# Hybrid GLA/MLA encoder layer: reciprocals by a small transpose, another order of loads and first products, and a root on GpSimd

## The chip, the cores and the metric

The kernel runs on one core of a Trainium2 chip. TensorE (PE) multiplies matrices, with weight loads (PEld) beside it; VectorE (DVE), ScalarE (ACT) and GpSimd (POOL) work on tiles in on-chip memory (SBUF) or in the matrix accumulators (PSUM); SyncE (SP) issues most of the DMA transfers, ACT a few. Each engine works through its own list in order and waits on semaphores. The metric is the time of one execution on the device in microseconds, as the median of several runs.

## The reference

One encoder layer over 2048 tokens of width 1024:

```python
h = x @ w_in
o_a = gla_branch(...)      # chunked gated linear attention, 4 heads, width 512
o_b = mla_branch(...)      # softmax attention on compressed keys and values, 4 heads, width 512
x = layer_norm(alpha * x + concatenate([o_a, o_b]) @ w_out, ln_g, ln_b)
```

In `mla_branch`, each query block takes `p = softmax(s)` over all 2048 keys, multiplies by the values and by `silu(gate)`. Everything is float32. The kernel keeps that precision by splitting each factor into a high part, rounded to TensorE's format, and the rest, and by taking three products (high by high, high by low, low by high) in `mm3`.

## The kernel before

The program has several sweeps over the tokens (input projections, the two scans of linear attention, the projections of the softmax branch), then the softmax attention, then the output projection with the layer norm. Only the last two are touched by the change. Tokens are taken in 16 chunks of 128 (`NCH`), queries in 4 blocks of 512 (`QB`).

**Attention.** There are 16 blocks `i`, one for each head and query block; block 15 is the last, block 14 the last but one. A block has eight steps `j`, each with two key tiles. `scores` fills a PSUM tile of `pS` (two buffers), ACT copies it (`copy`), VectorE keeps the running maximum (`smax`); after step 7, `tmax`, `rmax` and `bmax` turn the maximum into a row by transposes on TensorE with a reduction on VectorE between; `sub` (VectorE), `exp`, `phi` (ACT), `plo` (POOL) make the weights and `pv` multiplies them with the values into the bank `o`. `acc` sums the weights, and `tot` puts the sums into one tile; `tsum` transposes them on TensorE (tile `sx`), and `rcp` (VectorE) makes the reciprocals `rc`, 128 by 4. For block 15, `tot` is a copy out of the bank of the pool `pA`, and `tsum` and `y` borrow the banks `pA` and `pO` (`close`). `oh` and `ol` split `o`, `y` multiplies with the value projection, `yc` copies and stores the result in `ob_s`.

The reciprocals go to DRAM (`r_s`) in one of two ways. `keep` (L1639 to L1641) stores `rc` straight from its 128 by 4 tile, element by element, on ACT's queue. `turn` and `rows` (L1643 to L1654) first transpose it on TensorE into the bank `pA`, have ACT copy the four rows of 128, and store these on SP's queue. Before the change only block 15 takes the second way.

**Output stage.** For each chunk, `load` (L1839) fetches the two mixer outputs, the gate and the reciprocals; `hi` and `lo` (ACT, POOL) split the factors, `gate` (POOL, L1859) multiplies the softmax branch by gate and reciprocals, `load_res` (L1872) fetches the residual input `xr`; `part` and `product` take 48 matrix products of 512 columns; `residual` (VectorE, L1926) adds `alpha * xr` out of the bank, and `finish` (L1929) does the layer norm: mean and variance, `(r - mean) * gain` in two halves, the reciprocal root in `rsqrt` (logarithm and exponential on ACT, L432 and L433, then four one-column steps on VectorE, L438 to L441, which sharpen it), multiply-and-add in two halves (L1941) and two stores on SP's queue. Even chunks from 2 on use the banks `mb` and `x` (rows `pmb` and `px`), odd ones and chunks 0 and 1 use `pS` (rows `po`); so an even chunk can't start before `residual` has emptied the bank of the even chunk before it. The last chunk, 15, is taken in pieces of 512, 256 and 256 columns.

**What sets the order.** Attention and the first chunks are put in order by hand: `put(place, fn, ...)` gives each step a place, in units of a step `j` (`end` is 128, the end of the scores), and all engines follow the sorted list. The products of chunks 0 and 1 for each of the 8 weight tiles stand at `end + out["part"][k]`, `tmax` of block 15 at `end + 0.26`. Behind that list, chunks 4 to 15 run in a loop in which ACT, POOL and SP keep the written order (`fixed`, `LATE_ORDER`), while a planner orders TensorE and VectorE by priority and by when it expects inputs to be ready. In the loop, `split(c + 2)` is `hi`, `lo` and `gate` of a later chunk, `load(c + 4)` its loads, and the remaining steps of blocks 14 and 15 are appended behind chunks 4, 5 and 7.

Of the kernel before, what the change touches and what calls it, by code (L numbers as in the profile page):

```python
# [13 lines left out]
ALU = mybir.AluOpType  # L14
# [8 lines left out]
NCH = S // P  # L23
# [63 lines left out]
    tot=11.2,  # L87
    tsum=12.04,
    rcp=13.55,
    keep=14.21,  # L90
    oh=12.34,
    ol=12.99,
    y=16.55,
    yc=16.9,
# [20 lines left out]
    w_hi=0.74,  # L115
    w_step=6.49,
    w_lo=4.26,
    part=(1.05, 2.03, 5.45, 8.05, 10.24, 17.37, 21.96, 27.24),
    whole=(24.99, 55.73),
    sum=(38.16, 49.19),  # L120
# [234 lines left out]
class K:  # L355
# [77 lines left out]
        nc.scalar.activation(y, l, AF.Exp, scale=-0.5)  # L433
        return u, y, t, w, r

    def rsqrt_b(self, u, y, t, w, r):
        nc = self.nc
        nc.vector.tensor_tensor(t, y, u, ALU.mult)  # L438
        nc.vector.tensor_tensor(w, t, y, ALU.mult)
        nc.vector.tensor_scalar(t, w, -0.5, 1.5, ALU.mult, ALU.add)  # L440
        nc.vector.tensor_tensor(r, t, y, ALU.mult)  # L441
        return r

    def rsqrt(self, pool, u, n, name):
        return self.rsqrt_b(*self.rsqrt_a(pool, u, n, name))


    def load_w(self, pool, stage, src, ncols, tag, k, lo_eng="dve", hi_eng="act", bufs=None):
# [1037 lines left out]
    def attention(self):  # L1486
        tc, nc = self.tc, self.nc
        mm = nc.tensor.matmul
        V, G, Ac = nc.vector, nc.gpsimd, nc.scalar
        NP = NKT // 2  # L1490
        with ExitStack() as ctx:
# [6 lines left out]
            nb = len(blocks)  # L1498
# [140 lines left out]
            def keep(i):  # L1639
                h, b = blocks[i]  # L1640
                Ac.dma_start(self.r_s[b][:, h].rearrange("o (e p) -> p (o e)", p=P), stt[i]["rc"])  # L1641
# [46 lines left out]
            op = OutProj(self, ctx, qp, bp, sp, pS, pM, pX, pO, pA)  # L1688
            first = [dict(c=c) for c in range(4)]
# [4 lines left out]
            def put(place, fn, *a):  # L1694
                todo.append((place, len(todo), fn, a))
# [7 lines left out]
            for i in range(nb):  # L1703
                for j in range(NP):
                    t = NP * i + j
# [11 lines left out]
            out = PLACE_OUT  # L1717
            end = NP * nb
            for k in range(NK):
                if k < PRE_W:  # L1720
                    v = NP * (PRE_BLOCK + k)
                    hi, lo = v + out["pre_hi"], v + out["pre_lo"]
                else:
                    hi = end + out["w_hi"] + (k - PRE_W) * out["w_step"]
                    lo = hi + out["w_lo"]
                if k == 0:
                    put(hi - 6, op.fetch_w, k)
                put(hi, op.split_hi, k)
                put(lo, op.split_lo, k)
                if k + 1 < NK:  # L1730
                    put(lo + 0.01, op.fetch_w, k + 1)
                else:
                    put(max(lo, end + 26) + 0.02, op.load_ln)
                put(end + out["part"][k], lambda k: [op.part(o, k) for o in first[:2]], k)
            for c, o in enumerate(first):
                put(end + (out["lo1"][c - 1] + 0.01 if c else out["hi0"][0] - 6), op.load, o)
                for j in range(2):
# [16 lines left out]
            rest = {c: o for c, o in enumerate(first)}  # L1754

            def load(c):
                if c < NCH:
                    rest[c] = dict(c=c)
                    op.load(rest[c])

            def split(c):
                if c < NCH:
                    op.hi(rest[c], 0)
                    op.lo(rest[c], 0)
                    op.gate(rest[c])
                    op.hi(rest[c], 1)
                    op.lo(rest[c], 1)
# [17 lines left out]
                    op.finish(rest[c])  # L1785
            for c in range(4, NCH):
                with fixed():
                    split(c + 2)
                    load(c + 4)
                    if 4 < c < NCH - 1:  # L1790
                        op.load_res(rest[c + 1])
                    op.product(rest[c])
                    op.finish(rest[c])
                with self.after(*last.values()), fixed():
                    if c == 4:
                        keep(nb - 2)
                    for f in {4: (tot, oh, ol), 5: (tsum, rcp), 7: (turn, y, rows, yc)}.get(c, ()):
                        f(nb - 1)


class OutProj:
# [127 lines left out]
    def finish(self, o):  # L1929
        kern, nc, sm = self.k, self.nc, self.sm  # L1930
        V, Ac = nc.vector, nc.scalar
        c, rr = o["c"], o["rr"]
        mv = sm.tile([P, 2], F32, tag="mv", name=f"mv{c}")
        u = sm.tile([P, 1], F32, tag="u", name=f"u{c}")
        V.bn_aggr(mv, o["bn"])
        V.tensor_scalar(u, mv[:, 1:2], LN_EPS, None, ALU.add)
        for n in range(2):
            V.scalar_tensor_tensor(rr[:, n], rr[:, n], mv[:, 0:1], self.ln[0][:, n], ALU.subtract, ALU.mult)
        rs = kern.rsqrt(sm, u, 1, f"ln{c}")
        for n in range(2):  # L1940
            V.scalar_tensor_tensor(rr[:, n], rr[:, n], rs, self.ln[1][:, n], ALU.mult, ALU.add)  # L1941
            nc.sync.dma_start(kern.out[c * P:(c + 1) * P, n * 512:(n + 1) * 512], rr[:, n])
# [68 lines left out]
```

## Time and profile before

| What | Value |
|---|---|
| Median of 3 runs | 1307.95 us (1307.42 to 1308.66) |
| Profiled execution's own time | 1308.66 us |
| Its span | 1306.3 us |
| TensorE busy | 1280.9 us, 98% |
| VectorE busy | 958.2 us, 73% |
| ScalarE busy | 812.8 us, 62% |
| GpSimd busy | 783.6 us, 60% |

All rows give microseconds from the start of the span. A row of the timeline has start, duration, engine, line and operation, output and inputs, shapes and count, and in square brackets the idle time before it with what ended it; "x4" means that so many alike instructions are merged. In a list of waits, the three numbers are the sum, the count and the longest. A matmul of 512 columns is listed with its full length through the pipeline (0.39 us), while the next one follows in less; start to start is what counts. SPq and ACTq are the queues on which SP and ACT issue transfers: the duration of such a row is that of the issue, not of the transfer.

### The profile page before, as it was taken

What the parts mean: (1) busy time and instruction counts of PE and PEld (TensorE: products, weight loads), DVE (VectorE), ACT (ScalarE), POOL (GpSimd) and SP (SyncE); (2) the same over time, 40 slices, a digit from 0 to 9 for tenths busy, and PEclk for the clock granted to TensorE, in tenths of its full rate; (3) what the DMA queues carried; (4) which work ended last, traced back from release to release, by engine and by line L of the source; (5) the groups of instructions that cost most, each with busy time, mean ns of one, the idle gap of its engine ahead of it and who ended that gap; (6) DMA issues with size and microseconds to landing.
All of it is one profiled execution on the core that took longest, in us unless ns stands there. A gap on an engine that the chain in (4) does not pass through costs nothing.

```text
span 1306.3 us, 19979 instructions
## 1 busy us (share of the span) xinstructions
PE 1280.9 (98%) x7081; PEld 1130.9 (87%) x7081; DVE 958.2 (73%) x1712; ACT 812.8 (62%) x1339; POOL 783.6 (60%) x494
## 2 busy tenths in 40 slices
PE   7999999999999999999999999999999999999997
PEld 7999999999989999999788888888888887887786
DVE  6967774645675455555798888888888888377998
ACT  6764656655575656655688878888888888411110
POOL 0143333242457666672298888889999999934441
PEclk9999999999999999999999999999999999999999
DMA  8131313122475565565501111122123110376563
GB/s 285 61 101 54 94 49 91 55 68 79 132 249 170 193 214 181 178 210 170 145 1 41 41 42 41 41 57 65 58 81 97 41 41 12 119 234 175 195 197 109
DMA packets 107820, 145.81 MB, mean 112 GB/s; under 512 B 17251, under 2 KB 62695, under 8 KB 107721
## 3 DMA queue, kind: packets, MB, share of 16 engines
q1 hardware_dynamic: 99128, 142.41, 35.6%
q0 software_dynamic: 672, 2.10, 0.4%
q8 instruction: 56, 0.92, 0.3%
q10 hardware_dynamic: 7920, 0.03, 0.3%
q14 instruction: 44, 0.35, 0.2%
HBM read 94.14 MB, written 50.36 MB: 111 GB/s over the span
## 4 chain that ended last, share of the span: by engine, by line
PE 83%; DMA 4%; DVE 3%; ACT 2%; POOL 1%; issue 1%; SPq 1%; DVEq 0%; POOLq 0%; ACTq 0%
PE pS L1520 4%; PE o L419 4%; PE o L420 4%; PE o L421 4%; PE pS L1522 4%; PE pS L1523 4%; PE pS L1521 4%; PE pS L1524 4%; PE ipa L419 4%; PE ipa L421 4%; PE ipa L420 4%; PE pz L420 2%; PE pz L419 2%; PE pz L421 2%; PE ipg L419 2%; PE ipg L420 2%
## 5 line engine op out<-in xcount | busy, mean ns | idle before, releaser
L371 POOL TENSOR_TENSOR pl<-s,ph 128x1024 fp32r<-128x1024 f32 x128 | 306.5, 2414 | 58.3 <-ACT ph L365 54.5
L1542 DVE TENSOR_TENSOR rm<-pS,rm 128x512 f32<-128x512 f32 x210 | 144.8, 690 | 36.5 <-ACT s L1529 31.2
L1529 ACT ACTIVATE s<-pS 128x1024 f32<-128x1024 f32 x128 | 131.4, 1027 | 60.6 <-PE pS L1524 51.3
L1566 DVE TENSOR_TENSOR s<-s,mb 128x1024 f32<-128x1024 f32 x128 | 151.2, 1213 | 9.5 <-PE mb L1560 9.3
L1029 POOL TENSOR_TENSOR Us<-Us,cw 128x512 f32<-128x512 f32 x16 | 18.5, 1157 | 227.2 <-DVE Us L1027 175.3
L365 ACT ACTIVATE ph<-s 128x1024 fp32r<-128x1024 f32 x128 | 135.2, 1057 | 17.1 <-PE o L421 16.5
L1570 ACT ACTIVATE s<-s 128x1024 f32<-128x1024 f32 x128 | 131.4, 1050 | 13.7 <-DVE s L1566 13.7
L419 PE MATMUL ipa<-wah,xah 128*128 128x384 f32 (+1 forms) x384 | 131.1, 342 | 6.7 <-ACT wah L365 6.7
L421 PE MATMUL ipa<-wah,xal 128*128 128x384 f32 (+1 forms) x384 | 125.5, 327 | 0.0
L420 PE MATMUL ipa<-wal,xah 128*128 128x384 f32 (+1 forms) x384 | 125.2, 326 | 0.0
L1520 PE MATMUL pS<-qh,ckvT_h 128*128 128x512 f32 x256 | 102.6, 401 | 0.8 <-DVE rm L1542 0.4
L419 PE MATMUL o<-ph,vh 128*128 128x512 f32 x256 | 101.0, 395 | 0.0
L421 PE MATMUL o<-ph,vl 128*128 128x512 f32 x256 | 99.8, 390 | 0.0
L1522 PE MATMUL pS<-qh,ckvT_l 128*128 128x512 f32 x256 | 99.8, 390 | 0.0
L1523 PE MATMUL pS<-rh,krs 128*128 128x512 f32 x256 | 99.8, 390 | 0.0
L1524 PE MATMUL pS<-rl,krs 128*128 128x512 f32 x256 | 99.7, 389 | 0.0
L1521 PE MATMUL pS<-ql,ckvT_h 128*128 128x512 f32 x256 | 99.7, 389 | 0.0
L420 PE MATMUL o<-pl,vh 128*128 128x512 f32 x256 | 99.7, 389 | 0.0
L1593 DVE TENSOR_TENSOR ap<-ap,s 128x512 f32<-128x512 f32 x120 | 83.0, 692 | 2.7 <-ACT s L1570 0.7
L371 POOL TENSOR_TENSOR ol<-of,oh 128x512 fp32r<-128x512 f32 x32 | 42.9, 1343 | 66.9 <-ACT oh L365 66.9
L419 PEld LDWEIGHTS ipa<-wah,xah 128*128 128x128 f32 x384 | 73.7, 192 | 7.9 <-ACT wah L365 7.0
L419 PE MATMUL pz<-xch,wzh 128*128 128x256 f32 x256 | 74.8, 292 | 0.0
(325 smaller groups left out, 3858.0 us busy)
## 6 DMA issues: line engine op xcount, KB each, us to landing
xcf<-xT_dram SPq DMA_DIRECT2D x16, 512.0 KB, 4.9
xr<-x_dram SPq DMA_DIRECT2D x16, 512.0 KB, 6.6
out_dram<-rr SPq DMA_DIRECT2D x32, 256.0 KB, 2.0
xaf<-xT_dram SPq DMA_DIRECT2D x14, 512.0 KB, 4.2
oib<-oi_s SPq DMA_DIRECT2D x16, 256.0 KB, 4.4
qdb<-qd_s SPq DMA_DIRECT2D x16, 256.0 KB, 4.6
SU<-su_s SPq DMA_DIRECT2D x16, 256.0 KB, 4.9
ub<-u_s SPq DMA_DIRECT2D x16, 256.0 KB, 4.7
```

The costliest lines, as they stand in the source:

```text
L365: return nc.scalar.activation(dst, src, AF.Copy).ins
L371: return e.tensor_tensor(dst, src, hi.bitcast(F32), ALU.subtract).ins
L419: mm(out, ah, bh, start=start, stop=False)
L420: mm(out, ah, bl, start=False, stop=False)
L421: mm(out, al, bh, start=False, stop=stop)
L1520: mm(ps[:, e], kh, qh, start=True, stop=False)
L1521: mm(ps[:, e], kh, ql, start=False, stop=False)
L1522: mm(ps[:, e], kl, qh, start=False, stop=False)
L1523: mm(ps[:, e], kr, rh, start=False, stop=False)
L1524: mm(ps[:, e], kr, rl, start=False, stop=True)
L1542: V.tensor_tensor(d["rm"], src[:, e], d["rm"], ALU.max)
L1566: V.tensor_tensor(s, s, d["mb"][:, None, :].to_broadcast([P, 2, QB]), ALU.subtract)
```

## The change

1. The first two groups of products of the output stage, those of chunks 0 and 1 with weight tile 0, get places of their own: chunk 0's at `end + 0.255`, just before `tmax` of block 15 (0.26), chunk 1's stays at `end + 1.05`. Both stood at 1.05.
2. In the loop over chunks, `load_res` of the next chunk stands before `split` and `load` instead of behind them, for chunks 5 to 14. On SP's queue, one transfer passes four.
3. The reciprocals of block 14 no longer take `keep` but `turn` and `rows`, behind chunk 4: a transpose on TensorE into the bank `pA` after `tot` of block 15, a copy of 4 by 128 on ACT after `oh` of block 15, a store on SP's queue. One transfer of ACT's queue is gone.
4. The four one-column root steps of the last chunk run on GpSimd instead of VectorE.

```diff
@@ PLACE_OUT
+    part0=(0.255, 1.05),
     part=(1.05, 2.03, 5.45, 8.05, 10.24, 17.37, 21.96, 27.24),
@@ class K
-    def rsqrt_b(self, u, y, t, w, r):
-        nc = self.nc
-        nc.vector.tensor_tensor(t, y, u, ALU.mult)
-        nc.vector.tensor_tensor(w, t, y, ALU.mult)
-        nc.vector.tensor_scalar(t, w, -0.5, 1.5, ALU.mult, ALU.add)
-        nc.vector.tensor_tensor(r, t, y, ALU.mult)
+    def rsqrt_b(self, u, y, t, w, r, eng=None):
+        e = eng or self.nc.vector
+        e.tensor_tensor(t, y, u, ALU.mult)
+        e.tensor_tensor(w, t, y, ALU.mult)
+        e.tensor_scalar(t, w, -0.5, 1.5, ALU.mult, ALU.add)
+        e.tensor_tensor(r, t, y, ALU.mult)
         return r
-    def rsqrt(self, pool, u, n, name):
-        return self.rsqrt_b(*self.rsqrt_a(pool, u, n, name))
+    def rsqrt(self, pool, u, n, name, eng=None):
+        return self.rsqrt_b(*self.rsqrt_a(pool, u, n, name), eng)
@@ attention: the list by places
-                put(end + out["part"][k], lambda k: [op.part(o, k) for o in first[:2]], k)
+                for o, place in zip(first, out["part0"]):
+                    put(end + (out["part"][k] if k else place), op.part, o, k)
@@ attention: the loop over chunks
             for c in range(4, NCH):
                 with fixed():
+                    if 4 < c < NCH - 1:
+                        op.load_res(rest[c + 1])
                     split(c + 2)
                     load(c + 4)
-                    if 4 < c < NCH - 1:
-                        op.load_res(rest[c + 1])
                     op.product(rest[c])
                     op.finish(rest[c])
                 with self.after(*last.values()), fixed():
-                    if c == 4:
-                        keep(nb - 2)
-                    for f in {4: (tot, oh, ol), 5: (tsum, rcp), 7: (turn, y, rows, yc)}.get(c, ()):
-                        f(nb - 1)
+                    for f, i in {4: ((tot, 1), (turn, 2), (oh, 1), (ol, 1), (rows, 2)), 5: ((tsum, 1), (rcp, 1)),
+                                 7: ((turn, 1), (y, 1), (rows, 1), (yc, 1))}.get(c, ()):
+                        f(nb - i)
@@ OutProj.finish
-        rs = kern.rsqrt(sm, u, 1, f"ln{c}")
+        rs = kern.rsqrt(sm, u, 1, f"ln{c}", nc.gpsimd if c == NCH - 1 else V)
```

## The prediction

> **What bounds the kernel now.** I read the page first, then the waits of TensorE, then the chain of waits and the DMA issues of the stage that the diff touches.
>
> ```profile
> span 1306.3 us, 19979 instructions
> ...
> PE 1280.9 (98%) x7081; PEld 1130.9 (87%) x7081; DVE 958.2 (73%) x1712; ACT 812.8 (62%) x1339; POOL 783.6 (60%) x494
> ```
>
> TensorE is busy for 98% of the span, so only its gaps are to be had. Its list of waits from 1095 us to the end has two lines, one at the change from attention to output stage, one inside the output stage:
>
> ```profile
> PE pmb L419 <- DVE rr L1926: 3.1, 1, 3.1
> PE mx L1548 <- DVE rm L1542: 1.0, 1, 1.0
> ```
>
> The long one, in the chain that ended last (start, duration, what):
>
> ```profile
> 1185.22 14.26 DMA gr<-gm_s
> ...
> 1199.50 0.92 SPq L1853
> ...
> 1200.46 7.79 DMA xr<-x_dram
> ...
> 1208.38 0.70 DVE rr L1926
> ...
> 1209.22 0.47 PE pmb L419
> ```
>
> TensorE waits for VectorE to empty chunk 6's bank, VectorE for the residual input xr of chunk 6, and this stands on SP's queue behind the loads of chunk 9, which crawl. Why they crawl is in the DMA issues of 1180 to 1206 us, and what the gap leaves behind in the table of windows (PE busy, then other engines, then granted clock):
>
> ```profile
> r_s<-rc ACTq DMA_DIRECT2D x1, 2.0 KB, 11.0
> ```
>
> ```profile
> 1209.20:1213.00 3.80, 3.78 (x10) 2.96 (x11) 3.70 (x8) 0.92 (x3) 0.39 (x1) 0.56 0.77 238
> ```
>
> Two kilobytes of reciprocals, written element by element, take 11.0 us to land. And after the gap TensorE runs 3.80 us at a granted clock of 0.56, which loses (1 - 0.56) x 3.80 = 1.7 us more.
>
> **The change part by part.** The sum is made against the profiled execution's own 1308.66 us (span 1306.3, 2.4 around it); the median of the runs, 1307.95, is 0.7 less.
>
> Step 1, chunk 0's first six products ahead of the transposes `tmax`.
>
> ```profile
> 1097.74 0.39 PE L421 MATMUL o<-ph,vl 128*128 128x512 f32 x1
> 1099.10 0.63 PE L1548 MATMUL mx<-ident,rm 128*128 128x128 f32 x4 [0.97 <-DVE rm L1542]
> ```
>
> ```profile
> 1100.94 0.30 PEld L1560 LDWEIGHTS mb<-ident,mc 128*128 128x128 f32 x3 [0.25 <-DVE mc L1553]
> ```
>
> ```profile
> 1094.98 1.42 DVE L1542 TENSOR_TENSOR rm<-pS,rm 128x512 f32<-128x512 f32 x2 [0.76 <-ACT s L1529]
> 1097.54 1.42 DVE L1542 TENSOR_TENSOR rm<-pS,rm 128x512 f32<-128x512 f32 x2 [1.14 <-ACT s L1529]
> 1100.20 0.68 DVE L1553 TENSOR_REDUCE mc<-mx 128x4 f32<-128x512 f32 x1
> ```
>
> The bank that chunk 0 needs is the one of the last scores but one, free after the maximum that ends at 1094.98 + 1.42 = 1096.40, so the six products can issue from 1097.97 (0.23 after the row at 1097.74; 0.23 is also the spacing of the rows in step 3). They end at 1099.34. The transposes move from 1099.10 to 1099.34, the column maximum from 1100.20 to 1100.44, its end to 1101.12, and six products of attention fill TensorE until then. Both idle times go: 0.97 + 0.25 = 1.2 us. VectorE's subtractions for the last block start 0.24 later; TensorE waits for nothing between there and 1209, so that lateness is under cover of products already queued. If a producer that TensorE has so far met late-but-ready becomes the wait, the gain is given back: bounds -1.2 and 0, and I take -1.2.
>
> Step 2, xr ahead of the loads, and no element-wise store.
>
> ```profile
> 1190.79 1.00 SPq L1942 DMA_DIRECT2D out_dram<-rr  x2
> 1192.60 0.33 SPq L1850 DMA_DIRECT2D of<-oa_s  x1
> 1195.66 2.17 SPq L1851 DMA_DIRECT2D gr<-gm_s  x1
> ```
>
> ```profile
> SPq L1851 <- DMA r_s<-rc: 2.7, 1, 2.7
> ```
>
> ```profile
> 1197.60 1.42 DVE L1941 SCALAR_TENSOR_TENSOR rr<-rr,ln_r,lnb 128x512 f32<-128x512 f32 x2
> ```
>
> ```profile
> 1205.67 0.40 PE L421 MATMUL y<-ofh,wv_l 128*128 128x512 f32 x1
> ```
>
> SP is through with the stores of chunk 4 at 1191.79. The new order puts there one small store of the row form (0.3) and then xr, at about 1192.1 instead of 1200.46. Even with the 7.79 us that it took in the crawl it lands at 1199.9, and VectorE comes free of chunk 5 at 1199.02. So chunk 6's bank is empty by about 1201, and TensorE asks for it at 1205.9: 5 us of cover. The issue gap 1209.22 - 1205.67 - 0.23 = 3.3 us goes, and the 1.7 us of slow clock with it: -5.0. Bounds: -5.0, and -3.3 if the clock sags anyway. What is late next: the four loads of each chunk stand one issue (0.73 us or less) behind xr; they are made four chunks ahead of their products, and TensorE's list shows no wait for them. VectorE, which sat idle 9.4 us for xr, gets those back and doesn't become the bound. ACT's queue loses an issue, and ACT an idle 0.24 behind it (row at 1185.11 below).
>
> Step 3, a new wait. The transposed reciprocals of block 14 borrow the bank of the sums (`pA`), so `tsum` of block 15 now waits until ACT has copied them out, and ACT's written order puts that copy behind the root of chunk 4 and the copy `ofh` of block 15.
>
> ```profile
> 1182.65 0.39 PE L421 MATMUL po<-woh,ol 128*128 128x512 f32 x1
> 1182.88 0.60 PE L1629 MATMUL sx<-ident,acc 128*128 128x128 f32 x4
> ```
>
> ```profile
> 1184.67 0.20 ACT L433 ACTIVATE ln_y<-ln_l 128x1 f32<-128x1 f32 x1
> ...
> 1185.11 0.60 ACT L365 ACTIVATE ofh<-o 128x512 fp32r<-128x512 f32 x1 [0.24 <-issue]
> 1185.60 0.62 ACT L365 ACTIVATE oh<-of 128x512 fp32r<-128x512 f32 x1
> ```
>
> ```profile
> 1222.41 0.25 ACT L1653 ACTIVATE rt<-rt 4x128 f32<-4x128 f32 x1
> ```
>
> ```profile
> 1154.23 0.67 DVE L1614 COPY acc<-ap 128x512 f32<-128x512 f32 x1
> ```
>
> The sums' transposes are issued at 1182.88, right behind the last product of chunk 5. ACT ends chunk 4's root after that; `ofh` would start 0.24 sooner, at 1184.87, the copy 0.49 behind it (1185.60 - 1185.11) at 1185.36, with 0.25 of its own until 1185.61, and 0.14 to reach TensorE (VectorE's end 1098.96 to the transposes at 1099.10). So `sx` is issued at 1185.75: +2.9 us, with products of chunk 6 queued behind it. Step 1 moves TensorE and this chain alike, since the chain starts with xr of chunk 0, which waits for attention's products. Bounds: 0, if the planner puts the four transposes further down in chunk 6, and +4.6 with a slow clock behind the gap. I take +2.9, as the planner has `sx` directly behind chunk 5 now.
>
> Step 4, the transpose itself, one matmul behind chunk 4; its inputs are there since 1154.90 (the copy of the sums frees the bank).
>
> ```profile
> 1205.10 0.27 PE L1647 MATMUL rt<-ident,rc 128*4 128x128 f32 x1
> 1205.12 0.48 PE L419 MATMUL y<-ofh,wv_h 128*128 128x512 f32 x1
> ```
>
> Between 0.02 (the next issue) and 0.27 us; by the issue rows, 0.0.
>
> Step 5, the last root's four steps on GpSimd.
>
> ```profile
> 1300.10 0.20 ACT L433 ACTIVATE ln_y<-ln_l 128x1 f32<-128x1 f32 x1
> ```
>
> ```profile
> 1299.75 1.40 DVE L1938 SCALAR_TENSOR_TENSOR rr<-rr,mv,lng 128x512 f32<-128x512 f32 x2
> ...
> 1301.84 1.41 DVE L1941 SCALAR_TENSOR_TENSOR rr<-rr,ln_r,lnb 128x512 f32<-128x512 f32 x2
> ```
>
> ```profile
> L371 POOL TENSOR_TENSOR vl<-ckv,vh 128x128 fp32r<-128x128 f32 x16 | 7.4, 461 | 0.3 <-ACT vh L365 0.3
> L371 POOL TENSOR_TENSOR krs<-krf,krs 128x64 fp32r<-128x64 f32 x16 | 5.1, 318 | 1.0 <-ACT krs L365 1.0
> ```
>
> ```profile
> 1196.26 1.29 POOL L371 TENSOR_TENSOR ol<-of,oh 128x512 fp32r<-128x512 f32 x1 [3.69 <-ACT oh L365]
> ```
>
> ```profile
> 1196.52 1.05 DVE L441 TENSOR_TENSOR ln_r<-ln_t,ln_y 128x1 f32<-128x1 f32 x1
> ```
>
> The two GpSimd rows give 143 ns for 64 columns, so 318 - 143 = 0.18 us for one column; four steps with about 0.07 between them (an estimate, half the hop of step 3) and the hop back take 1.0 us. Begun at 1300.30, when the exponential ends, they would let VectorE start the final multiply at 1301.3 instead of 1301.84: -0.5. But VectorE's second multiply by the gain runs until 1301.15, and the last two rows show a one-column product on VectorE that ends with GpSimd's operation (1197.57 and 1197.55): the two engines take turns. If GpSimd is the one that waits, 1301.15 + 1.0 = 1302.15: +0.3. Those rows are the nearest: +0.3. The Trainium skill's page SBUF — State Buffer (SBUF: two separate sides) speaks against this step: whichever of a two-input VectorE operation and a GpSimd operation starts first holds the shared ports for its whole length. By that rule it is +0.3, without it -0.5; rows and rule agree for the case where VectorE waits, and the reverse case is in no run here.
>
> Sum: -1.2 - 5.0 + 2.9 + 0.0 + 0.3 = -3.0, or 1305.7 in the profiled execution's terms and **1304.9 us** as a median (-0.23%).
>
> **The rivals.**
> A: no wait in step 3, because the planner sends `sx` down into chunk 6 or the copy comes in time: -5.9, so 1302.0. Against it: `sx` stands behind chunk 5 now, and nothing but the bank holds it.
> B: the gap of step 3 slows the clock. It would be 2.7 us of idle where 3.15 did it; the same 1.7 us more gives 1306.7. The gaps of 0.97 and 0.25 did not. The Trainium skill's page TensorE: Matmul & The Clock Gate (What's actually happening) gives an idle window of about 3.4 us as what throttles the clock. By that figure this gap would leave the clock alone and the sum stays; the row above, where a shorter gap already slowed it, makes me keep B.
> C: step 1 gives nothing, the 1.2 us being handed back to the next late producer: 1306.1.
> D, slower: the root steps are GpSimd's first multiply-and-add by constants and its last work, with only 0.85 us of VectorE's multiply (to 1301.15) as cover. GpSimd has been late for no visible reason before:
>
> ```profile
> 103.38 1.36 POOL L1029 TENSOR_TENSOR Us<-Us,cw 128x512 f32<-128x512 f32 x1 [11.86 <-issue]
> ```
>
> Such an idle time here would end the steps at 1300.30 + 11.86 + 1.0 = 1313.2, 11.0 behind my 1302.15: 1315.9. It makes the kernel slower by over 0.2% once the steps end after 1307.7 (1302.15 + 3.0 + 2.6). Against it: that row may hide an ordinary wait, and GpSimd's other operations start promptly. The Trainium skill's page GPSIMD Engine Reference (Instruction dispatch) gives about 6 us for the first call of freshly loaded code; by that the sum would be 1310.9, and no run here shows it.
>
> **How the numbers follow.** My forecast 0.45, A 0.25, B 0.17, C 0.05, D 0.08. The runs can tell about 0.2%, 2.6 us, from no change; my forecast lies just past it, so two thirds of its chance go to faster and one third to same. Faster: 0.30 + 0.25 = 0.55 and 0.02 of B; same: 0.15 + 0.14 + 0.05 = 0.34; slower: 0.08 and 0.01 of B. The range runs from A with the tail at -0.5 (1301.2) to B (1306.8); D is left out. All but D are faster or same; the forecast's own range is 1304 to 1306.
>
> **What would show it.** Step 1: no wait before `mx`, po rows ahead of it. Step 2: no wait before chunk 8's pmb, no window with a low clock near 1209, xr of chunk 6 landing before 1200. Step 3: a wait of 2 to 3 us before `sx`, ended by ACT's `rt` copy; if it is absent, A holds. Step 5: four POOL rows at the end, the first of which begins late or lasts until VectorE is done. I am wrong if a further wait shows on TensorE, or if the final multiply starts much later behind the start of the last exponential than the 1.74 us of now (1301.84 - 1300.10).

## The result and the profile after

The changed kernel takes 1305.74 us as the median (1303.26 to 1307.79), against 1308.14 us for the kernel before in the same comparison: ratio 0.9981, 95% interval 0.9975 to 0.9987. That is 2.4 us faster. The forecast was 1304.9 us and 0.23%. In a second comparison, on another chip (e11 below), it took 1305.95 us against 1306.58: 0.6 us less, with an interval that holds no change at all. The profiled execution of the changed kernel took 1305.01 us of its own, 3.65 less than that of before.

The page of the changed kernel:

```profile
span 1302.7 us, 19980 instructions
...
PE 1277.7 (98%) x7082; PEld 1128.9 (87%) x7082; DVE 961.2 (74%) x1708; ACT 812.5 (62%) x1340; POOL 785.6 (60%) x498
```

TensorE's list of waits from 1090 us to the end has one line where there were two. Lines of kernel.py stand one further down than before.

```profile
PE sx L1630 <- ACT rt L1654: 2.2, 1, 2.2
```

Both old waits are gone and the new one of step 3 is there. TensorE's timeline gives the place of each gain (start, duration, instruction):

```profile
1097.81 0.39 PE L422 MATMUL o<-ph,vl 128*128 128x512 f32 x1
1098.04 0.39 PE L420 MATMUL po<-woh,oh 128*128 128x512 f32 x1
...
1099.40 0.60 PE L1549 MATMUL mx<-ident,rm 128*128 128x128 f32 x4
...
1181.69 0.39 PE L422 MATMUL po<-woh,ol 128*128 128x512 f32 x1
1184.32 0.66 PE L1630 MATMUL sx<-ident,acc 128*128 128x128 f32 x4 [2.24 <-ACT rt L1654]
...
1207.19 0.40 PE L422 MATMUL y<-ofh,wv_l 128*128 128x512 f32 x1
1207.42 0.39 PE L420 MATMUL pmb<-woh,oh 128*128 128x512 f32 x1
...
1294.68 0.28 PE L422 MATMUL pap<-woh,ol 128*128 128x256 f32 x1
```

Before, the last product was issued here:

```profile
1298.18 0.28 PE L421 MATMUL pap<-woh,ol 128*128 128x256 f32 x1
```

The last attention product ahead of the touched place was issued at 1097.74 before and at 1097.81 after, so 0.07 is taken off each later difference: chunk 5 ends 1182.65 - 1181.69 + 0.07 = 1.0 us earlier, `sx` is issued 1184.32 - 1182.88 - 0.07 = 1.4 later, chunk 8 starts 1209.22 - 1207.42 + 0.07 = 1.9 earlier, and the last product comes 3.6 earlier. The gap before chunk 8 is gone (0.23 between the rows at 1207.19 and 1207.42), and with it the slow clock; the clock also stays at 1.00 behind the new wait, in this execution:

```profile
1184.70:1188.50 3.80, 3.80 (x20) 3.15 (x19) 3.70 (x5) 0.09 (x1) 3.55 (x3) 1.00 0.87 239
...
1207.40:1211.20 3.80, 3.80 (x18) 3.13 (x17) 3.69 (x5) 0.63 (x1) 2.91 (x3) 1.00 0.29 92
```

xr of chunk 6 is issued 9.6 us earlier than before, and the two residual inputs between 1180 and 1206 take 3.8 us to land where one took 7.8:

```profile
1190.82 0.36 SPq L1873 DMA_DIRECT2D xr<-x_dram  x1
```

```profile
xr<-x_dram SPq DMA_DIRECT2D x2, 512.0 KB, 3.8
```

The chain that ended last now runs through the new wait:

```profile
1180.75 2.35 DVE rr L1942 x2
1183.11 0.07 DVE u L1937
...
1183.20 0.21 ACT ln_l L433
...
1183.44 0.20 ACT ln_y L434
1183.64 0.48 ACT ofh L366
1184.12 0.16 ACT rt L1654
...
1184.32 0.66 PE sx L1630 x4
```

VectorE still works off chunks 3 and 4, so the variance of chunk 4 (`u`) is late, ACT's root waits for it, and the copy `rt` stands behind the root and behind `ofh` in ACT's written order. TensorE finished chunk 5 two microseconds earlier.

### The profile page after: what moved, and what is told of

It reads as the page before. It is cut to its first block, busy times and chain, and to the rows that moved or that the text cites. A ratio compares the mean times of both kernels' runs of the same rounds, so it can differ in the third digit from the quotient of the medians.

```text
span 1302.7 us, 19980 instructions
## 1 busy us (share of the span) xinstructions
PE 1277.7 (98%) x7082; PEld 1128.9 (87%) x7082; DVE 961.2 (74%) x1708; ACT 812.5 (62%) x1340; POOL 785.6 (60%) x498
## 4 chain that ended last, share of the span: by engine, by line
PE 84%; DVE 3%; ACT 2%; POOL 2%; DMA 2%; issue 1%; SPq 1%; DVEq 0%; POOLq 0%; ACTq 0%
PE o L420 4%; PE o L421 4%; PE o L422 4%; PE pS L1521 4%; PE pS L1522 4%; PE pS L1523 4%; PE pS L1524 4%; PE pS L1525 4%; PE ipa L420 4%; PE ipa L422 4%; PE ipa L421 4%; PE pz L421 2%; PE pz L422 2%; PE pz L420 2%; PE po L422 2%; PE po L421 2%
```

## The experiments

One measure serves for all profiles: the stage, from the issue of the last attention product ahead of the touched place to that of the last product of chunk 15. It leaves out the rest of the program: that attention product is issued anywhere between 1096.66 and 1099.08 us after the start in these profiles, whatever the kernel. Gap is TensorE's wait before `sx` or before chunk 8's `pmb`, clock that of the 3.8 us behind it. The ratio is to the kernel before, timed on the same chip. The experiments ran on three chips, on which the kernel before took 1306.64 us (e1 to e4), 1306.62 (e5 to e8) and 1306.58 (e9 to e12), 1.5 us less than in the first comparison; so ratios can be compared across the table, and medians within one of these groups.

| Kernel | Median us | Ratio (95%) | Stage us | Gap us | Clock |
|---|---|---|---|---|---|
| before | 1308.14 | 1 | 200.44 | 3.15, chunk 8 | 0.56 |
| before, second profile (e7) | 1308.31 (one run) | | 199.34 | 2.08, chunk 8 | 0.66 |
| changed | 1305.74 | 0.9981 (0.9975 to 0.9987) | 196.87 | 2.24, sx | 1.00 |
| changed, second profile (e8) | 1306.59 (one run) | | 198.08 | 1.86, sx | 0.57 |
| changed, timed again (e11) | 1305.95 | 0.9994 (0.9985 to 1.0002) | 196.62 | 2.01, sx | 1.00 |
| e1, first products alone | 1305.35 | 0.9992 (0.9983 to 1.0002) | 196.73 | 2.22, chunk 8 | 1.00 |
| e2, order of loads alone | 1303.17 | 0.9974 (0.9966 to 0.9983) | 195.44 | none | |
| e3, small transpose alone | 1307.82 | 1.0013 (1.0004 to 1.0022) | 197.75 | 1.96, sx | 1.00 |
| e4, copy ahead of chunk 4 | 1302.13 | 0.9967 (0.9955 to 0.9978) | 194.37 | none | |
| e5, element-wise store back | 1300.88 | 0.9959 (0.9946 to 0.9972) | 194.22 | none | |
| e12, the same again | 1301.88 | 0.9966 (0.9954 to 0.9979) | 194.24 | none | |
| e6, root back on VectorE | 1305.72 | 0.9992 (0.9981 to 1.0002) | 198.33 | 2.10, sx | 0.58 |
| e9, copy before ofh | 1304.00 | 0.9984 (0.9976 to 0.9993) | 196.39 | 1.78, sx | 1.00 |
| e10, copy behind oh of chunk 7 | 1306.67 | 0.9997 (0.9988 to 1.0006) | 198.75 | 2.56, sx | 0.55 |

**First products alone (e1).**

```diff
 # the kernel before
+    part0=(0.255, 1.05),
...
-                put(end + out["part"][k], lambda k: [op.part(o, k) for o in first[:2]], k)
+                for o, place in zip(first, out["part0"]):
+                    put(end + (out["part"][k] if k else place), op.part, o, k)
```

> The kernel before with step 1 alone: chunk 0's first six products ahead of the transposes of the last maximum. My theory (TensorE's idle time there is filled and nothing later takes it back): no wait before mx, the last product of chunk 5 about 1.0 us earlier, the later gap of 3.1 us before chunk 8 and its slow clock as they are; about 1.0 us faster, ratio 0.9992. Rival (the earlier arrival is handed back at the next late producer): mx without a wait, but the end within 0.3 us of before.

The wait before `mx` is gone, and TensorE's only wait is the old one:

```profile
PE pmb L420 <- DVE rr L1928: 2.2, 1, 2.2
```

By medians it is 1.3 us faster, with an interval that holds the expected 1.0 us and also zero. The old gap is 2.2 us long here instead of 3.15, and no slow clock followed it, against what was expected; so the stage, 3.7 us shorter, holds more than step 1. Step 1 by itself can be read at the last product of chunk 5: it is issued 84.91 us after the stage's start before (1182.65 - 1097.74) and 83.70 in e1 (1180.69 - 1096.99), 1.2 us earlier.

**Order of loads alone (e2).**

```diff
 # the kernel before
                 with fixed():
+                    if 4 < c < NCH - 1:
+                        op.load_res(rest[c + 1])
                     split(c + 2)
                     load(c + 4)
-                    if 4 < c < NCH - 1:
-                        op.load_res(rest[c + 1])
```

> The kernel before with the residual input ahead of the loads alone; the element-wise store stays. My theory (the gap before chunk 8 comes from the place of xr on SP's queue): xr of chunk 6 is issued near 1192 instead of 1200.5, lands by about 1200 even beside the element-wise store, no wait before chunk 8's pmb and none before sx; 3.3 us of gap and 1.7 us of slow clock go, about 5.0 us faster, ratio 0.9962. Rival (the element-wise store itself is the cause, it holds up whatever is in flight): xr crawls too, lands after 1205, and the wait before chunk 8 stays in good part; less than 2 us faster.

The stage is 5.0 us shorter than in the profile of before, with no wait left but the old one before `mx`:

```profile
PE mx L1548 <- DVE rm L1542: 1.0, 1, 1.0
```

xr is issued beside the element-wise store and does crawl, so both theories had a point. It lands in time all the same: SP's issue, its time to landing, and VectorE's use of it, which TensorE needs by about 1205.8:

```profile
1191.41 1.43 SPq L1872 DMA_DIRECT2D xr<-x_dram  x1
```

```profile
xr<-x_dram SPq DMA_DIRECT2D x1, 512.0 KB, 11.9
```

```profile
1203.47 0.69 DVE L1926 SCALAR_TENSOR_TENSOR rr<-xr,pmb 128x512 f32<-128x512 f32 x1 [4.74 <-DMA xr<-x_dram]
```

I had expected the landing by 1200; it was 1203.3, and the margin is 1.6 us (1205.8 less the end of that row at 1204.16). By medians e2 is 3.5 us faster than before. Its stage is 1.2 to 2.6 us shorter than those of the changed kernel; the two were not timed on one chip, and their ratios (0.9974 against 0.9981 and 0.9994) only lean the same way. The order removes the old gap by itself.

**Small transpose alone (e3).**

```diff
 # the kernel before
-                    if c == 4:
-                        keep(nb - 2)
-                    for f in {4: (tot, oh, ol), 5: (tsum, rcp), 7: (turn, y, rows, yc)}.get(c, ()):
-                        f(nb - 1)
+                    for f, i in {4: ((tot, 1), (turn, 2), (oh, 1), (ol, 1), (rows, 2)), 5: ((tsum, 1), (rcp, 1)),
+                                 7: ((turn, 1), (y, 1), (rows, 1), (yc, 1))}.get(c, ()):
+                        f(nb - i)
```

> The kernel before with block 14's reciprocals by the small transpose alone; the loads keep their order. My theory (two effects of opposite sign): the loads of chunk 9 no longer crawl, xr of chunk 6 is issued near 1195 and lands near 1201, so the gap before chunk 8 goes with its slow clock (-5.0), and a wait of 2.4 us before sx appears, ended by ACT's copy rt; about 2.6 us faster, ratio 0.9980. Rival (the order is what counts): the wait before chunk 8 stays, the wait before sx is added; 0 to 2.4 us slower.

```profile
PE sx L1629 <- ACT rt L1653: 2.0, 1, 2.0
PE mx L1548 <- DVE rm L1542: 1.0, 1, 1.0
```

The mechanism is as expected: the old gap is gone, the new one is there, and the stage is 2.7 us shorter than in the first profile of before. So the wait before chunk 8 needs both the old order and the element-wise store; taking away either removes it. But the forecast of 2.6 us faster failed: by medians this kernel is 1.2 us slower. Its profiled execution, 1306.16 us, was the fastest of all of its executions, with full clock behind the gap; 1.7 us more for a slow clock gives the median, 1307.8. And against the second profile of before (e7: gap 2.08 us, slow clock, stage 199.34) the stage with 1.7 us added, 199.4, would be no gain. That the slow clock came in most executions of e3 is argued, not shown.

**ACT's copy ahead of chunk 4 (e4).**

```diff
 # the changed kernel
+                if c == 4:
+                    with self.after(*last.values()), fixed():
+                        tot(nb - 1)
+                        turn(nb - 2)
+                        rows(nb - 2)
+                with fixed():
                     op.product(rest[c])
                     op.finish(rest[c])
...
-                    for f, i in {4: ((tot, 1), (turn, 2), (oh, 1), (ol, 1), (rows, 2)), 5: ((tsum, 1), (rcp, 1)),
+                    for f, i in {4: ((oh, 1), (ol, 1)), 5: ((tsum, 1), (rcp, 1)),
```

> The changed kernel with the sums' copy, the transpose of block 14's reciprocals and ACT's copy of them put ahead of chunk 4's products and root, so that ACT has them out of the bank before chunk 5 ends. Everything is computed. My theory (the wait before sx is ACT's order, not the transpose): no wait before sx, 2.4 us faster than the changed kernel, 4.9 us faster than before (ratio 0.9963 by the medians of the two kernels, 0.9955 by their profiled executions). Rival (TensorE's gain is limited further on by VectorE or a later load): the wait shows up again before another bank of chunks 6 to 10, and the time stays near that of the changed kernel, ratio 0.998.

TensorE's list of waits from 1090 us on is empty, and the stage is 194.37 us, 2.5 less than that of the changed kernel. The transpose is still there and the wait is not, so the wait was ACT's order, and nothing further on takes the gain back. By medians e4 is 4.5 us faster than before (4.9 expected).

**Element-wise store back (e5, e12).**

```diff
 # the changed kernel
-                    for f, i in {4: ((tot, 1), (turn, 2), (oh, 1), (ol, 1), (rows, 2)), 5: ((tsum, 1), (rcp, 1)),
+                    if c == 4:
+                        keep(nb - 2)
+                    for f, i in {4: ((tot, 1), (oh, 1), (ol, 1)), 5: ((tsum, 1), (rcp, 1)),
```

> The changed kernel with the element-wise store on ACT's queue back in place of the small transpose; order of loads, first products and last root as changed. My theory (with xr ahead of the loads the element-wise store does no harm on the path that sets the end, and without the shared bank there is no wait before sx): no wait of TensorE from 1095 us on, about 2.4 us faster than the changed kernel, ratio to before 0.9963. Rival (the element-wise store delays xr or the loads of chunk 8 enough to matter): a wait before chunk 8 or chunk 9 of 1 us or more, time at or above that of the changed kernel, ratio 0.998 or more.

```profile
span 1298.9 us, 19978 instructions
```

No wait of TensorE from 1090 us on, and the shortest stage of all. It was timed a second time, on one chip with the changed kernel:

> The changed kernel with the element-wise store back, on the same chip as the changed kernel. Expected from its first run: no wait of TensorE over 0.2 us from 1095 us on, single times within about 2.5 us, ratio to before 0.996, that is 2 to 4 us below the changed kernel of the same call. Rival (the first runs were lucky): within 1 us of the changed kernel.

> The changed kernel on the same chip as its three variants, for a direct comparison. Expected: ratio to before 0.998, a wait near 2 us before sx, single times spread over 3 to 4 us.

1301.88 us against 1305.95 us: 4.1 us less, with all of its single times (1300.92 to 1303.41) below all of the other's (1303.57 to 1307.39). This version beats both kernels. The changed kernel's own second ratio is 0.9994, lower in gain than the first, with 1 inside its interval.

**Root back on VectorE (e6).**

```diff
-        rs = kern.rsqrt(sm, u, 1, f"ln{c}", nc.gpsimd if c == NCH - 1 else V)
+        rs = kern.rsqrt(sm, u, 1, f"ln{c}", V)
```

> The changed kernel with the last root's four steps back on VectorE. My theory from the two profiles (1.74 us from the last exponential's start to the final multiply before, 1.68 after): 0.1 us slower than the changed kernel, not to be told from it, ratio to before 0.998. Rival (GpSimd's steps cost a late start in most executions, and the one profile was lucky): faster than the changed kernel by 0.3 us or more.

The last exponential (ACT) and the final multiply (VectorE) of this kernel:

```profile
1297.62 0.20 ACT L434 ACTIVATE ln_y<-ln_l 128x1 f32<-128x1 f32 x1
```

```profile
1299.35 0.75 DVE L1942 SCALAR_TENSOR_TENSOR rr<-rr,ln_r,lnb 128x512 f32<-128x512 f32 x1
```

From the one to the other 1.73 us, against 1.68 in the changed kernel (rows in the next section). The medians can't tell a difference of that size, and e6 and the changed kernel were timed on different chips.

**Second profiles (e7, e8).**

> The kernel before once more, for a second profile. Expected: the wait before chunk 8 is 3.1 us again, give or take 1 us of the loads' landing. Theory (a gap of this length always slows the clock): a stretch at about half clock behind it, 1.7 us lost. Rival (it depends on where the gap falls): full clock behind the same gap, which would make the kernel before 1.7 us faster in such executions and explain why the runs' medians lie 2.4 us apart and the two profiled executions 3.6.

> The changed kernel once more, for a second profile. Expected: the wait of 2.2 us before sx again. Theory (a gap of this length leaves the clock alone): full clock behind it. Rival: in this execution the clock sags behind it, 1.7 us lost, which would explain why the changed kernel's median lies above its profiled execution.

The kernel before and its window behind the gap:

```profile
PE pmb L419 <- DVE rr L1926: 2.1, 1, 2.1
```

```profile
1208.90:1212.70 3.80, 3.75 (x11) 3.02 (x12) 3.70 (x8) 0.93 (x3) 0.35 (x1) 0.66 0.73 231
```

The changed kernel:

```profile
PE sx L1630 <- ACT rt L1654: 1.9, 1, 1.9
```

```profile
1184.70:1188.50 3.80, 3.80 (x13) 3.04 (x12) 3.69 (x5) 0.06 (x1) 3.59 (x3) 0.57 0.84 239
```

The same program has full clock behind a gap of 2.24 us in one execution and 0.57 behind 1.86 us in another. So the rival on the clock happened, in part of the executions. And the gap of before was 3.15 us in one profile and 2.08 in the other.

**The copy one place earlier and one later (e9, e10).**

```diff
 # e9
-                    ... (turn, 2), (oh, 1), (ol, 1), (rows, 2) ...
+                    ... (turn, 2), (rows, 2), (oh, 1), (ol, 1) ...
 # e10: rows(nb - 2) taken out there, and in split
                 op.hi(rest[c], 0)
+                if c == 7:
+                    rows(nb - 2)
                 op.lo(rest[c], 0)
```

> The changed kernel with ACT's copy of block 14's transposed reciprocals one place further ahead, before the copy ofh of block 15 instead of behind it. My theory (the wait before sx is exactly ACT's order): the wait falls by the 0.47 us that ofh holds ACT, from about 2.1 to about 1.6. Theory on the clock (a gap near 2 us sags the clock in some executions, by chance of where it falls, and a shorter gap does so less often): time 0.5 to 1.3 us below the changed kernel, and most single times within 1.5 us of each other. Rival (the sag doesn't depend on the gap's length): 0.5 us below it, with the changed kernel's spread of 4 us.

> The changed kernel with the same copy one place further back, behind the first copy oh of chunk 7. My theory: the wait before sx grows by that copy's 0.49 us, to about 2.6. Theory on the clock: slow in nearly every execution, so 0.5 us from the gap and up to 0.9 us from more frequent sags, 0.5 to 1.4 us above the changed kernel. Rival (sag independent of the length): 0.5 us above it.

The last exponential of chunk 4's root (ACT) and the transposes `sx` (TensorE), first e9, then e10:

```profile
1183.40 0.20 ACT L434 ACTIVATE ln_y<-ln_l 128x1 f32<-128x1 f32 x1
1183.81 0.66 PE L1630 MATMUL sx<-ident,acc 128*128 128x128 f32 x4 [1.78 <-ACT rt L1654]
```

```profile
1184.48 0.20 ACT L434 ACTIVATE ln_y<-ln_l 128x1 f32<-128x1 f32 x1
1185.89 1.08 PE L1630 MATMUL sx<-ident,acc 128*128 128x128 f32 x4 [2.56 <-ACT rt L1654]
```

The wait follows ACT's place for the copy. From the start of the exponential to `sx` it is 0.41 us in e9, 0.88 to 0.90 in the three profiles of the changed kernel and 1.41 in e10: about half a microsecond less and more, as expected. The length of the wait (1.8; 1.9 to 2.2; 2.6) also depends on when the exponential comes, so that e9's alone would not be clear of the changed kernel's.

Against the changed kernel on the same chip the medians are 1.95 us lower and 0.7 higher. The first is more than was expected of either theory, the second fits both. Nine of e9's eleven single times lie within 1.44 us, as the theory on the clock had it.

**What the traces say of the clock.** By length the gaps don't part: 1.78, 1.96, 2.01, 2.22 and 2.24 us left the clock alone, and 1.86, 2.08, 2.10, 2.56 and 3.15 did not. But in all 14 profiles the times between two changes of the granted clock are whole multiples of 3.413 us (in e8 343 at full clock, one at half, 33 at full, then the drop behind the end), so each execution has a grid of such periods. Windows cut along it (behind the length TensorE's busy time, as the third last number the granted clock), first e8, then the changed kernel (its grid counted back from the drop at 1299.13):

```profile
1181.83:1185.24 3.41, 1.55 (x9) 1.06 (x8) 3.41 (x7) 1.56 (x5) 1.10 (x2) 1.00 0.58 182
1185.25:1188.65 3.40, 3.40 (x9) 2.63 (x8) 3.29 (x4) 0.00 (x0) 3.32 (x3) 0.50 0.84 254
1188.67:1192.07 3.40, 3.40 (x16) 2.81 (x15) 3.40 (x6) 0.63 (x1) 1.66 (x2) 1.00 0.64 187
```

```profile
1179.67:1183.08 3.41, 2.41 (x11) 1.68 (x9) 3.41 (x8) 0.63 (x1) 2.14 (x2) 1.00 0.21 78
1183.08:1186.49 3.41, 2.17 (x12) 1.86 (x13) 3.34 (x9) 1.56 (x5) 1.62 (x2) 1.00 0.72 217
```

In e8 the whole gap of 1.86 us lies in one period, and the next runs at half clock; in the changed kernel a longer gap is cut into 1.00 and 1.24 us, and the clock stays up. The most idle time that a gap left in one period parts all ten without exception: 1.24 (changed), 1.37 (e3), 1.44 (e1), 1.78 (e9) and 1.80 us (e11) at full clock, 1.86 (e8), 2.08 (e7), 2.10 (e6), 2.56 (e10) and 2.96 (before) with a slow period behind. So by these profiles what decides is where the gap falls on the grid, which lies differently in each execution; a gap of 1.8 us or less can't leave more than that in one period, wherever it falls. This is read from the profiles afterwards; no run was made to test it.

## Why the prediction was right, and where its sizes were off

*Step 1, -1.2.* Measured -1.2 at the end of chunk 5 in e1, where it stands alone; the -1.0 in the changed kernel holds step 4 as well. The transposes moved to 1099.40, 0.23 later once the 0.07 is taken off (0.24 forecast), and both idle times went. Rival C, nothing gained, didn't happen.

*Step 2, -5.0.* In the pair of profiles 3.3 us of gap and 1.7 of clock went, as forecast (1.9 earlier at chunk 8 plus the 1.4 of lateness at `sx` is 3.3; 3.6 at the end against 1.9 is 1.7). The cause named was right: e2, with the order alone, has no wait before chunk 8. What was mis-sized is the term as a typical value. It came from one execution with a long gap and a slow clock; the gap was 2.08 us in e7, with a slow clock, and 2.22 in e1, where the clock stayed up. Without a slow clock and with a gap of 2.2, the step is worth some 2.4 us instead of 5.0. My lower bound of 3.3 took the gap's length as fixed.

*Step 3, +2.9.* Measured +2.4 in that pair, a wait of 1.9 to 2.2 us, ended by the instruction named. The 0.24 us of idle time behind ACT's issue went as assumed, and a little more: `ofh` starts 0.11 us behind the exponential's start (1183.44 to 1183.55 in ACT's timeline), where I had 0.20. Chunk 4's root also moved further ahead than TensorE did: the exponential by 1.3 us (from 86.93 to 85.63 us after the stage's start), chunk 5's end by 1.0. The hop to TensorE was shorter than the 0.14 I took (0.04 in the chain). Rival A, no wait at all, didn't happen; e4 shows what it would have given. Rival B did, in some executions: 0.57 in e8, 0.58 in e6. I had priced it well (1.7 us; the range's upper end, 1306.8, should have been its 1306.7) and made it a case of its own, where each execution can meet it, by where the gap falls on the clock's grid. The Trainium skill's page TensorE: Matmul & The Clock Gate (What's actually happening) names an idle window of about 3.4 us as what throttles the clock. The traces agree with the window's length, 3.413 us, but 1.86 us of idle time in one were enough here, so the measurement decides.

That the medians moved 2.4 us and the two first profiles 3.6 fits this: the profile of before had the longer gap and the slow clock, the profile after had the full clock. Kernels without a gap have narrow single times (1.0 to 2.7 us from lowest to highest in e2, e4, e5 and e12), those with one wider (3.7 to 4.9 in the changed kernel and its other variants). The mean clock of whole executions agrees, though it is rounded to 0.001 and one slow period lowers it by 0.0013: of the first 22 executions of the changed kernel, the seven with 0.999 took 1303.26 to 1305.01 us and the seven with 0.997 took 1305.72 to 1307.37, and none of the 26 without a gap is below 0.998. How often each kernel meets the slow clock can't be counted exactly this way, so the split of the 2.4 us among the steps is argued, not shown. That it came so near to the forecast 3.0 is partly luck: the sum had a slow clock in step 2 and none in step 3, as the two first profiles happened to have, and the second comparison gave 0.6.

*Step 4, 0.0.* Measured 0.1 to 0.2. Up to the end of chunk 5 the transpose of block 14's reciprocals is all that sets e3 apart on TensorE, and its chunk 5 ends at 85.04 us of the stage instead of 84.91; with step 1 it is 83.86 to 83.88 in the kernels with the transpose and 83.67 to 83.73 in those without (e1, e5, e12). The rows of the changed kernel show where: the product behind the transpose is followed only after 0.32 us instead of 0.23. I had looked at the first of these spacings (0.02) alone.

```profile
1170.89 0.27 PE L1648 MATMUL rt<-ident,rc 128*4 128x128 f32 x1
1170.91 0.48 PE L420 MATMUL po<-woh,oh 128*128 128x512 f32 x1
1171.23 0.40 PE L421 MATMUL po<-wol,oh 128*128 128x512 f32 x1
```

*Step 5, +0.3.* Measured -0.06 in one pair of profiles (1.68 us against 1.74; e6, with the steps on VectorE, 1.73). ACT's exponential, VectorE's neighbours and GpSimd's four steps:

```profile
1296.61 0.20 ACT L434 ACTIVATE ln_y<-ln_l 128x1 f32<-128x1 f32 x1
```

```profile
1296.26 1.40 DVE L1939 SCALAR_TENSOR_TENSOR rr<-rr,mv,lng 128x512 f32<-128x512 f32 x2
1298.29 1.42 DVE L1942 SCALAR_TENSOR_TENSOR rr<-rr,ln_r,lnb 128x512 f32<-128x512 f32 x2 [0.63 <-POOL ln_r L442]
```

```profile
1296.88 0.19 POOL L439 TENSOR_TENSOR ln_t<-ln_y,u 128x1 f32<-128x1 f32 x1 [23.25 <-ACT ln_y L434]
1297.15 0.56 POOL L440 TENSOR_TENSOR ln_t<-ln_t,ln_y 128x1 f32<-128x1 f32 x1
1297.80 0.18 POOL L441 TENSOR_SCALAR ln_t<-ln_t 128x1 f32<-128x1 f32 x1
1298.07 0.19 POOL L442 TENSOR_TENSOR ln_r<-ln_t,ln_y 128x1 f32<-128x1 f32 x1
```

The price of a step, 0.18 us, was right, and GpSimd did wait for VectorE: the second step lasts 0.56 us and ends at 1297.71, 0.05 behind VectorE's second multiply (1297.66). What I had wrong is that the first step is held as well; it got through at 1296.88, so only three steps were left. The Trainium skill's page SBUF — State Buffer (SBUF: two separate sides), by which the operation that starts first holds the shared ports for its whole length, agrees with the second step; the first it doesn't settle. Rival D, a late start on GpSimd, didn't show: 0.07 us from the exponential's end to the first step, and 0.18 us for the multiply-and-add by constants, its first in the kernel.

## What to carry to other kernels

When a transfer that an engine waits for stands on a queue behind others that wait or crawl, move it ahead first: that alone (e2) gave a shorter stage than the whole change. A bank that is borrowed for a new small step makes the bank's next user wait for the step's reader, at the place where that reader stands in its engine's order; here moving the copy ahead (e4), or not borrowing the bank (e5), gave 2 to 4 us more. And a gap seen in one profile has a length and a clock of that one execution: for a change of 2 in 1300, look at a second profile before you size it, and see whether the slow clock behind a gap comes in every execution.

## What the runs showed of the hardware

- The granted clock changes on a grid of 3.413 us. A period in which TensorE sat idle for 1.86 us or more was followed by one at half clock (0.50), which costs up to 1.7 us; with 1.80 us or less it was not. This holds for all ten gaps of 1.78 to 3.15 us, five on each side. None of the four profiles without such a gap has a slow period ahead of the last product.
- A store of 2 KB by single elements takes 11.0 us to land (10.8 in e2), and half a megabyte issued beside it 11.9 us (e2) instead of 3.8. Yet TensorE had no wait behind it in e2, e5 and e12, where what it needed had been issued early enough.
- A one-column operation on GpSimd took 0.18 to 0.19 us where VectorE didn't hold it, and the next one that depends on it started 0.08 to 0.09 us after it ended.
